# Second MLP product begun inside the first one's last pair, its second block product's loads and sums spread over steps

## The chip, the core and the metric

The kernel runs on one core of one Trainium2 chip, as one program and one launch. The metric is the device time of an execution in microseconds, taken as the median of several runs. The engines named below are TensorE (PE, matrix products), VectorE (DVE), ScalarE (ACT), GpSimd (POOL) and SyncE (SP), which issues all the DMAs that matter here.

## What is computed

The reference is a two-layer transformer trunk over 1024 latent tokens of width 1024 (an attention layer, then a gated-convolution layer). Each layer ends with the same kind of MLP, and the change lies in these two:

```python
def sq_relu_mlp(h, w1, w2):
    return jnp.square(jax.nn.relu(h @ w1)) @ w2

h = modulate(x, sh2, sc2)
x = layer_norm(DEEPNORM_ALPHA * x + g2 * sq_relu_mlp(h, mlp_w1[l], mlp_w2[l]), ln_g[l, 1], ln_b[l, 1])
```

Here `h` is 1024 x 1024, `w1` is 1024 x 4096 and `w2` is 4096 x 1024, all in float32.

## The kernel before

**Three matmuls for one.** Every product is made with operands split into a high part rounded to fp32r and a low part that is the rest. `mm3` (lines 72 to 75) issues high x high (line 73), one mixed product (line 74) and the other mixed product (line 75) into the same PSUM bank. A split is a cast on ACT (high part) and a subtraction on DVE (low part, line 78).

**Seven block products for eight.** Most of both MLP products is done by a Strassen-Winograd scheme: a 2 x 2 block product from seven block products, numbered x = 1 to 7, of sums of blocks.

**First product (`mlp_in`, line 721).** Four of the 32 row blocks of `w1` are multiplied plainly. The other 28 go in 14 pairs, p = 0 to 13. For each pair `quarters` (line 803) loads two row blocks, splits them, and runs the seven block products (n = 0 to 6, 12 matmuls each). After the squared ReLU, `mlp_in` stores the seven combinations that the second product needs in DRAM tensors `gq`, by DMAs at line 757. `between(n)` is called after each block product n.

**Second product (`merged`, line 860, called by `dense_out`).** It runs over seq: for x in the order 1, 6, 7, 4, 2, 5, 3, fourteen K tiles p = 0 to 13. One (x, p) is called a step here. A step is four times `mm3`, 12 matmuls of 128 x 512, into four PSUM banks (j = 0 to 3), in which all 14 steps of one x add up; x = 6 goes on in the banks of x = 1. `plus(x)` (line 925) then adds each of the four banks to the accumulator `acc`, once its last matmul is done. With x = 1 the fourteen steps are numbered 0 to 13 in this text, with x = 6 they are 14 to 27.

What a step needs is prepared two steps earlier by `ahead(n)`:

- `load` (line 894): 128 x 512 blocks of `w2` (256 KB): `a11`, `a21`, `a22`, later `a12`. Before step 0 `ahead(0)` asks for all 14 of `a11` and then all 28 of `a21` and `a22`.
- `make_b` (lines 903 to 906), for every second step: loads `b` from `gq` (512 KB, two K tiles) and splits it into `bh` (ACT, line 905) and `bl` (DVE, line 78).
- `make_a` (line 912): forms the block sum that this x wants (line 913), and splits it into two halves of a `part` tile: ACT cast at line 916, DVE subtraction at line 78. For x = 6 the sums are a21 = a11 - a21 and a22 = a22 - a21; x = 5 later wants a11 = a11 + a22.

`part`, `bh` and `bl` share a ring of six tiles with the split operands of `quarters`. Between `mlp_in` and `dense_out` the pool of temporaries changes (`small("x")`), whose tiles lie where the first product's temporaries were.

**What sets the order.** A tile scheduler places each engine's instructions in one queue per engine, as soon as it believes them ready, near the order in which the code issues them. Instructions wrapped in `keep_in_program_order` keep their places among each other: the casts and subtractions of `make_a` and `make_b` are wrapped, the block sums of line 913 are not. `high_priority(offset=60)` lets the four additions of `plus` move ahead. SP's queue holds all loads and stores. `gate_rows` (lines 195 to 206) is issued at step (2, 0): eight copies on DVE (`spread`, line 202) and eight PE transposes (line 203) that have no inputs from this product.

Of the kernel before, what the change touches and what calls it, by code (L numbers as in the profile page):

```python
# [55 lines left out]
class Trunk:  # L56
# [659 lines left out]
    def mlp(self, l, norm):  # L716
        self.g = [self.dp.tile([P, T], F32, name="g", tag="g", bufs=8) for _ in range(4)]
        self.gq = [{x: self.dp.tile([P, T], F32, name="gq", tag="gq", bufs=2 * 49) for x in range(1, 8)} for _ in range(7)]
        self.small("v")
        self.mlp_in(l)  # L720
        self.small("x")
        self.dense_out(self.w2[l], (self.m0, self.m1)[l], 40, norm)

    def mlp_in(self, l):

        nc = self.nc
        w1 = [self.weight(self.w1[l, m]) for m in range(4)]
        for h in range(2):  # L730
            for m in range(4):
                ps = self.gemm_in(w1[m], h * H2)
                r = self.tmp()
                nc.scalar.activation(r, ps, AF.Relu)
                nc.vector.scalar_tensor_tensor(out=r, in0=ps, scalar=0.0, in1=r, op0=ALU.max, op1=ALU.mult)
                self.leave(r, m, h)
                if h == 1:
                    self.combine(m)
        left = list(range(48)) if l == 0 else []
        if left:  # L740
            cb = self.raw("cb3")
            self.rows(cb, self.act[:, 0:8])

        def adaln():
            if left:
                i = left.pop(0)
                raw = self.raw()
                nc.sync.dma_start(out=raw, in_=self.adaT[1, i * P:(i + 1) * P, :])
                self.ada_dot(raw, cb, self.m1[:, i:i + 1], raw)
                if not left:  # L750
                    nc.vector.tensor_tensor(out=self.m1, in0=self.m1, in1=self.cols_t[:, C_ADAB + 48:C_ADAB + 96], op=ALU.add)

        for p in range(14):
            b = {}

            def leave(x, t):
                nc.sync.dma_start(out=self.gq[p // 2][x][:, p % 2 * H2:(p % 2 + 1) * H2], in_=t)

            def square(i, h, c, src):
                nc.scalar.activation(c, src, AF.Relu)  # L760
                nc.scalar.activation(c, c, AF.Square)
                b[i, h] = c
                if (i, h) != (0, 1):
                    leave({(0, 0): 1, (1, 0): 2, (1, 1): 3}[i, h], c)

            def between(n):
                if n % 2 == 1 or n == 6:
                    adaln()

            self.quarters([self.w1[l, 4 + 2 * p], self.w1[l, 5 + 2 * p]], square, between)  # L770

            def diff(a, c, op=ALU.subtract, out=None):
                out = out or self.tmp()
                nc.vector.tensor_tensor(out=out, in0=a, in1=c, op=op)
                return out

            b12 = diff(b[1, 1], b[0, 1], out=b[0, 1])
            leave(7, b12)
            b11 = diff(b[0, 0], b12, ALU.add)
            leave(6, b11)  # L780
            leave(5, diff(b[1, 1], b11))
            leave(4, diff(b[1, 0], b11))
# [91 lines left out]
    def merged(self, w, bs, k0, mod, gcol, step):  # L874

        nc = self.nc
        g = mod[:, gcol:gcol + 8]  # L880
        pairs = range(2 * len(bs))
# [27 lines left out]
                bparts[x, 2 * pp + i] = hi[:, c], lo[:, c]  # L909

        def make_a(x, p):
            for o, a, b, f in sums.get(x, ()):
                nc.vector.tensor_tensor(out=q[o, p], in0=q[a, p], in1=q[b, p], op=f)
            src = q[use[x], p]
            hi, lo = self.hl("part")
            self.tc.keep_in_program_order(nc.scalar.copy(out=hi, in_=src))  # L916
# [3 lines left out]
        def plus(x):  # L920

            for j, t in enumerate(ps[x]):
                jj, h = {1: (j, 0), 6: (j, 1), 7: (4 + j, 1), 4: (4 + j, 0), 2: (j, 0), 5: (4 + j, 1), 3: (j, 1)}[x]
                acc = self.acc[jj, h]
                nc.vector.scalar_tensor_tensor(out=acc, in0=t, scalar=g[:, jj:jj + 1], in1=acc, op0=ALU.mult, op1=ALU.add)

        def ahead(n):

            x, p = seq[n]
            if n == 0:  # L930
                for pp in pairs:
                    load("a11", pp)
                for pp in pairs:
                    load("a21", pp)
                    load("a22", pp)
            if x == 6:
                load("a12", p)
            if x == 4:
                load("a22", p, "a22r")
            if p % 2 == 0:  # L940
                make_b(x, p // 2)
            make_a(x, p)

        for n in range(-2, len(seq)):
            if n + 2 < len(seq):
                ahead(n + 2)
            if n < 0:
                continue
            x, p = seq[n]
            on = x in (6, 7, 4, 3)  # L950
            if p == 0:
# [13 lines left out]

    def dense_out(self, w, mod, gcol, norm):

        nc = self.nc

        def step(x, p):  # L970
# [3 lines left out]
                self.centre(norm[0], 0)  # L974

        if self.gq:
            self.merged(w, self.gq, len(self.g), mod, gcol, step)
        nchunk = len(self.g) // 4
        for c in range(nchunk):
            hid = {}  # L980
# [16 lines left out]
    def conv(self):  # L997
# [92 lines left out]
            self.quarters([self.cw_in[j], self.cw_in[j + 1]], gates)  # L1090
        self.small("x")
        self.gq = []
        self.dense_out(self.cw_out, self.m1, 16, (2, (self.m1, 3)))


class Attention:
# [202 lines left out]
class Grouped:  # L1299
# [154 lines left out]
    def ahead(self, j, m):  # L1454
        with self.t.tc.high_priority(offset=40):
            if m < 8:
                self.maximum(j, m // 2, m % 2)
            if m == 8:
                self.shifts(j)
# [58 lines left out]
```

## Time and profile before

| | before |
|---|---|
| median of 3 runs | 2580.47 us (2570.87 to 2581.67) |
| profiled execution, its own time | 2576.91 us |
| its span, first to last instruction | 2575.1 us |
| mean granted TensorE clock | 0.974 |
| PE busy / weight loads / DVE / ACT / POOL | 95% / 74% / 73% / 48% / 13% |

PE is busy for 95% of the span, so time can only be gained where PE waits or where its clock is granted at half. The table of 40 slices of the page shows such slices at several places: in the attention part, at the layer norms, and at the two changes from the first MLP product to the second (about 1200 to 1250 us in layer 0 and 2213 to 2252 us in layer 1). A granted clock of 1.00 is 2.4 GHz, the lower level is 1.2 GHz.

### The profile page before, as it was taken

The page shows a single profiled execution, that of the slowest core. Times are in us where ns is not written, and L with a number is a line of the kernel's source. Part 1 is how long each engine was busy: PE and PEld are TensorE (multiplying, and loading weights), DVE is VectorE, ACT ScalarE, POOL GpSimd, SP SyncE. Part 2 cuts the span into 40 slices and gives each one's busy share as a digit, 9 for nine tenths or more (in the row PEclk, how much of TensorE's full clock was granted, in tenths as well). Part 3 has the DMA queues.
Part 4 walks back from the last instruction along what each step waited for, and adds up shares of the span by engine and source line. Part 5 has one row for each costly group of instructions (what it writes and reads, how often), then busy time and mean ns, then how long its engine had stood idle before and what let it go on. Part 6 is the DMA issues. An engine that isn't in the chain of part 4 may idle for free. (4 is left out here: it accounts for less than half of the span.)

```text
span 2575.1 us, 30269 instructions
## 1 busy us (share of the span) xinstructions
PE 2435.0 (95%) x10950; PEld 1895.7 (74%) x10950; DVE 1891.7 (73%) x2925; ACT 1225.9 (48%) x1986; POOL 345.2 (13%) x230
## 2 busy tenths in 40 slices
PE   7999899999999979999899999999999999899997
PEld 5888677744447767787688777788777888688786
DVE  4847888887768787876756689767887565765867
ACT  3113577755542475554344346534258555344343
POOL 0001000044442410000000033001231000000002
PEclk9999899999999989999899999999999999899999
DMA  7811011000011057877542221123213444843231
GB/s 271 288 52 46 21 21 46 15 16 6 1 66 50 21 177 250 258 270 257 197 150 88 94 103 33 58 82 120 102 33 126 141 151 160 308 136 132 88 117 66
DMA packets 118519, 297.15 MB, mean 115 GB/s; under 512 B 13536, under 2 KB 19296, under 8 KB 118368
## 3 DMA queue, kind: packets, MB, share of 16 engines
q1 hardware_dynamic: 118368, 295.20, 34.2%
q8 instruction: 86, 1.41, 0.2%
q14 instruction: 65, 0.53, 0.1%
HBM read 225.29 MB, written 63.96 MB: 112 GB/s over the span
## 5 line engine op out<-in xcount | busy, mean ns | idle before, releaser
L74 PE MATMUL ps<-bl,part 128*128 128x512 f32 x784 | 309.7, 396 | 7.0 <-DVE bl L78 7.0
L73 PE MATMUL ps<-bh,part 128*128 128x512 f32 x784 | 310.4, 397 | 6.2 <-ACT part L916 6.2
L75 PE MATMUL ps<-bh,part 128*128 128x512 f32 x784 | 308.7, 396 | 5.8 <-DVE part L78 5.8
L916 ACT CAST part<-a 128x512 fp32r<-128x512 f32 x196 | 121.7, 623 | 306.5 <-PE ps L74 159.8
L78 DVE TENSOR_TENSOR part<-a,part 128x512 fp32r<-128x512 f32 x196 | 134.7, 690 | 162.1 <-ACT part L916 162.1
L73 PE MATMUL ps<-T,a 128*128 128x512 f32 x608 | 238.6, 392 | 6.4 <-DVE tmp L825 3.6
L74 PE MATMUL ps<-T,a 128*128 128x512 f32 x608 | 237.5, 391 | 2.2 <-DVE T L78 2.2
L75 PE MATMUL ps<-T,a 128*128 128x512 f32 x608 | 237.2, 390 | 0.0
L536 POOL TENSOR_TENSOR acc<-acc,mb 128x512 f32<-128x512 f32 x29 | 48.1, 1688 | 1070.6 <-ACT mb L533 1070.6
L73 PE MATMUL ps<-H,a 128*128 128x512 f32 x456 | 178.5, 392 | 3.7 <-ACT a L540 3.7
L74 PEld LDWEIGHTS ps<-bl,part 128*128 128x128 f32 x784 | 150.2, 192 | 41.1 <-DVE bl L78 9.2
L78 DVE TENSOR_TENSOR a<-raw,a 128x1024 fp32r<-128x1024 f32 (+1 forms) x114 | 119.2, 1047 | 83.3 <-PE ps L74 72.5
L75 PEld LDWEIGHTS ps<-bh,part 128*128 128x128 f32 x784 | 150.3, 192 | 38.7 <-DVE part L78 7.2
L73 PEld LDWEIGHTS ps<-bh,part 128*128 128x128 f32 x784 | 149.8, 191 | 39.3 <-ACT part L916 7.4
L74 PE MATMUL ps<-H,a 128*128 128x512 f32 x456 | 177.9, 390 | 0.0
L75 PE MATMUL ps<-H,a 128*128 128x512 f32 x456 | 177.7, 390 | 0.0
L540 ACT CAST a<-raw 128x1024 fp32r<-128x1024 f32 (+1 forms) x114 | 100.9, 908 | 136.2 <-PE ps L74 94.6
L825 DVE TENSOR_TENSOR tmp<-ps,tmp 128x512 f32<-128x512 f32 x114 | 78.4, 689 | 116.0 <-PE ps L75 80.2
L73 PEld LDWEIGHTS ps<-T,a 128*128 128x128 f32 x608 | 114.4, 188 | 35.3 <-DVE tmp L825 6.2
L74 PEld LDWEIGHTS ps<-T,a 128*128 128x128 f32 x608 | 114.4, 188 | 26.6 <-DVE T L78 3.6
L75 PEld LDWEIGHTS ps<-T,a 128*128 128x128 f32 x608 | 114.6, 188 | 23.9
L1390 ACT ACTIVATE pt<-s 128x512 f32<-128x512 f32 x160 | 92.7, 596 | 81.0 <-PE s L1389 72.1
(414 smaller groups left out, 5907.0 us busy)
## 6 DMA issues: line engine op xcount, KB each, us to landing
gq<-tmp SPq DMA_DIRECT2D x196, 256.0 KB, 3.4
b<-gq SPq DMA_DIRECT2D x98, 512.0 KB, 3.3
raw<-in_w SPq DMA_DIRECT2D x72, 512.0 KB, 4.2
a<-in_w SPq DMA_DIRECT2D x140, 256.0 KB, 5.1
raw<-in_adaT SPq DMA_DIRECT2D x48, 512.0 KB, 5.0
adar<-in_adaT SPq DMA_DIRECT2D x32, 512.0 KB, 5.0
raw<-in_cw_in SPq DMA_DIRECT2D x24, 512.0 KB, 3.6
ada<-in_adaN SPq DMA_DIRECT2D x16, 512.0 KB, 8.4
```

Source lines behind the costliest of these rows:

```text
L73: mm(ps, lhsT=lh, rhs=rh, start=start, stop=False, **kw)
L74: mm(ps, lhsT=lh, rhs=rl, start=False, stop=False, **kw)
L75: mm(ps, lhsT=ll, rhs=rh, start=False, stop=stop, **kw)
L78: return eng.tensor_tensor(out=out, in0=a, in1=hi.bitcast(F32), op=ALU.subtract)
L536: self.eng(NORM[li, h]["sub"][j]).tensor_tensor(out=a, in0=a, in1=mb, op=ALU.subtract)
L540: self.nc.scalar.copy(out=hi, in_=src)
L825: nc.vector.tensor_tensor(out=o, in0=a, in1=b, op=op)
L916: self.tc.keep_in_program_order(nc.scalar.copy(out=hi, in_=src))
L1390: nc.scalar.activation(pt[:, s, :], o, AF.Exp)
```

## The change

- `dense_out` and `merged` become generators. `merged` issues `ahead(0)` and `ahead(1)` and then yields; `mlp` runs it up to there from `between(5)` of the last pair (p = 13), and runs the rest after `small("x")`. The other caller of `dense_out`, in `conv`, runs it through at once.
- `ahead(0)` issues the 14 loads of `a11` alone. The loads of `a21` and `a22` for K tile p are issued by the step of x = 1 that prepares p.
- `make_b` is issued ahead of the loads in `ahead`.
- The difference a21 = a11 - a21 is issued by `differences`, wrapped in `keep_in_program_order`: one in each x = 1 step from p = 3 on, and one in each of the first x = 6 steps until none is left. The difference a22 = a22 - a21 is issued in `make_a` of x = 6 and is wrapped as well; the sum for x = 5 is not.

No instruction is added or removed; all of them move.

```diff
         self.small("v")
-        self.mlp_in(l)
+        out = self.dense_out(self.w2[l], (self.m0, self.m1)[l], 40, norm)
+        self.mlp_in(l, lambda: next(out))
         self.small("x")
-        self.dense_out(self.w2[l], (self.m0, self.m1)[l], 40, norm)
-
-    def mlp_in(self, l):
+        for _ in out:
+            pass
+
+    def mlp_in(self, l, then):
...
             def between(n):
                 if n % 2 == 1 or n == 6:
                     adaln()
+                if p == 13 and n == 5:
+                    then()
...
         def make_a(x, p):
-            for o, a, b, f in sums.get(x, ()):
-                nc.vector.tensor_tensor(out=q[o, p], in0=q[a, p], in1=q[b, p], op=f)
+            for o, a, b, f in sums.get(x, ())[x == 6:]:
+                i = nc.vector.tensor_tensor(out=q[o, p], in0=q[a, p], in1=q[b, p], op=f)
+                if x == 6:
+                    self.tc.keep_in_program_order(i)
...
+        early = []
+
+        def differences(n):
+
+            for _ in range(n):
+                p = early.pop(0)
+                o, a, b, f = sums[6][0]
+                self.tc.keep_in_program_order(nc.vector.tensor_tensor(out=q[o, p], in0=q[a, p], in1=q[b, p], op=f))
+
         def ahead(n):
 
             x, p = seq[n]
+            if p % 2 == 0:
+                make_b(x, p // 2)
             if n == 0:
                 for pp in pairs:
                     load("a11", pp)
-                for pp in pairs:
-                    load("a21", pp)
-                    load("a22", pp)
+            if x == 1:
+                make_a(x, p)
+                if p > 2:
+                    differences(1)
+                load("a21", p)
+                load("a22", p)
+                early.append(p)
+                return
             if x == 6:
                 load("a12", p)
+                if early:
+                    differences(1)
             if x == 4:
                 load("a22", p, "a22r")
-            if p % 2 == 0:
-                make_b(x, p // 2)
             make_a(x, p)
 
-        for n in range(-2, len(seq)):
+        for n in range(2):
+            ahead(n)
+        yield
+        for n in range(len(seq)):
             if n + 2 < len(seq):
                 ahead(n + 2)
-            if n < 0:
-                continue
...
         if self.gq:
-            self.merged(w, self.gq, len(self.g), mod, gcol, step)
+            yield from self.merged(w, self.gq, len(self.g), mod, gcol, step)
...
-        self.dense_out(self.cw_out, self.m1, 16, (2, (self.m1, 3)))
+        for _ in self.dense_out(self.cw_out, self.m1, 16, (2, (self.m1, 3))):
+            pass
```

The built programs differ only around the two changes from the first product to the second, and alike in both layers. Three places follow, all of layer 0.

ACT at the end of the first product, before: the last squared ReLUs of pair 13 (lines 760 and 761), then the casts for steps 0 to 2.

```order
L760 ACTIVATE tmp_10180<-tmp_10180 128x512
L761 ACTIVATE tmp_10180<-tmp_10180 128x512
L760 ACTIVATE tmp_10165<-tmp_10165 128x512
L761 ACTIVATE tmp_10165<-tmp_10165 128x512
L760 ACTIVATE tmp_10225<-ps_10121 128x512
L761 ACTIVATE tmp_10225<-tmp_10225 128x512
L905 CAST bh_10330<-b_10328 128x1024
L916 CAST part_10334<-a11_10244 128x512
L916 CAST part_10337<-a11_10246 128x512
```

ACT at the same place, changed (lines 762 and 763 are now the squared ReLU, 910 and 923 the casts).

```order
L762 ACTIVATE tmp_10180<-tmp_10180 128x512
L763 ACTIVATE tmp_10180<-tmp_10180 128x512
L910 CAST bh_10212<-b_10210 128x1024
L923 CAST part_10244<-a11_10216 128x512
L923 CAST part_10251<-a11_10218 128x512
L762 ACTIVATE tmp_10165<-tmp_10165 128x512
L763 ACTIVATE tmp_10165<-tmp_10165 128x512
L762 ACTIVATE tmp_10273<-ps_10121 128x512
L763 ACTIVATE tmp_10273<-tmp_10273 128x512
L910 CAST bh_10294<-b_10292 128x1024
```

The three casts for steps 0 and 1 now stand ahead of the last two squared ReLUs. On DVE the subtractions for steps 0 and 1 moved likewise, ahead of the last four combinations of the first product.

SP, the loads of `w2` blocks and of `b` for x = 1, before. `b_10416` is the `b` of steps 6 and 7; the `b` of steps 0 to 5 were issued earlier.

```order
L894 DMA a21_10324<-in_w2 128x512
L894 DMA a22_10326<-in_w2 128x512
L903 DMA b_10416<-gq_7644 128x1024
L903 DMA b_10452<-gq_7651 128x1024
L903 DMA b_10492<-gq_7658 128x1024
L903 DMA b_10528<-gq_7665 128x1024
L894 DMA a12_10564<-in_w2 128x512
```

SP at the same place, changed (line 899 loads blocks, line 908 loads `b`).

```order
L899 DMA a21_10371<-in_w2 128x512
L899 DMA a22_10373<-in_w2 128x512
L908 DMA b_10387<-gq_7644 128x1024
L899 DMA a21_10397<-in_w2 128x512
L899 DMA a22_10399<-in_w2 128x512
L899 DMA a21_10417<-in_w2 128x512
L899 DMA a22_10419<-in_w2 128x512
L908 DMA b_10433<-gq_7651 128x1024
```

The `b` of steps 6 and 7 stood behind all 28 loads of `a21` and `a22`; now it stands behind 12 of them, and each later `b` four loads further. Behind the first product's last five stores those are the last 25 before and 8 now.

DVE at the change from x = 1 to x = 6, before: the low part of step 14 (`part_10574`) stands ahead of the four additions of `plus(1)`, and the differences are long done; line 913 is by now the sum for x = 5.

```order
L78 TENSOR_TENSOR part_10549<-a11_10270,part_10549 128x512
L913 TENSOR_TENSOR a11_10270<-a11_10270,a22_10326 128x512
L78 TENSOR_TENSOR bl_10569<-b_10566,bh_10568 128x1024
L78 TENSOR_TENSOR part_10574<-a22_10274,part_10574 128x512
L925 SCALAR_TENSOR_TENSOR acc_6762<-ps_10349,m0_63,acc_6762 128x512
L925 SCALAR_TENSOR_TENSOR acc_6768<-ps_10350,m0_63,acc_6768 128x512
L925 SCALAR_TENSOR_TENSOR acc_6774<-ps_10351,m0_63,acc_6774 128x512
L925 SCALAR_TENSOR_TENSOR acc_6780<-ps_10352,m0_63,acc_6780 128x512
L78 TENSOR_TENSOR part_10593<-a22_10278,part_10593 128x512
```

DVE at the same place, changed (line 941 is the difference a21, line 918 the sums in `make_a`, line 932 `plus`).

```order
L941 TENSOR_TENSOR a21_10513<-a11_10238,a21_10513 128x512
L932 SCALAR_TENSOR_TENSOR acc_6762<-ps_10305,m0_63,acc_6762 128x512
L932 SCALAR_TENSOR_TENSOR acc_6768<-ps_10306,m0_63,acc_6768 128x512
L932 SCALAR_TENSOR_TENSOR acc_6774<-ps_10307,m0_63,acc_6774 128x512
L932 SCALAR_TENSOR_TENSOR acc_6780<-ps_10308,m0_63,acc_6780 128x512
L918 TENSOR_TENSOR a22_10249<-a22_10249,a21_10247 128x512
L918 TENSOR_TENSOR a11_10216<-a11_10216,a22_10249 128x512
L78 TENSOR_TENSOR part_10585<-a22_10249,part_10585 128x512
L941 TENSOR_TENSOR a21_10539<-a11_10240,a21_10539 128x512
L918 TENSOR_TENSOR a22_10256<-a22_10256,a21_10254 128x512
L918 TENSOR_TENSOR a11_10218<-a11_10218,a22_10256 128x512
L78 TENSOR_TENSOR part_10604<-a22_10256,part_10604 128x512
```

The sum and the low part of step 14 now stand behind the four additions, and every x = 6 step has two block sums in the queue ahead of its low part. Behind these rows come the `bl` of steps 16 and 17, the last difference a21, and the sum a22 of step 16. On PE the eight transposes of `gate_rows` stood together between steps 5 and 6; four of them still do, the other four now stand between steps 13 and 14.

## Rows read from the trace of the kernel before

**Rows 1.** Busy time by stretch: us, PE, PEld, DVE, ACT, POOL, PEclk, DMA share, GB/s.

```profile
1200.00:1225.00 25.00, 22.00 (x84) 16.88 (x82) 20.94 (x33) 8.85 (x13) 0.00 (x0) 0.86 1.01 356
1225.00:1250.00 25.00, 17.31 (x58) 12.77 (x59) 20.75 (x37) 6.38 (x9) 0.00 (x0) 0.73 0.68 258
```

**Rows 2.** Timeline of PE, both product changes: start, length, line, tiles, count [idle before, releaser].

```profile
1201.90 0.39 PE L75 MATMUL ps<-T,a 128*128 128x512 f32 x1
1205.09 1.65 PE L73 MATMUL ps<-bh,part 128*128 128x512 f32 x3 [2.80 <-ACT part L916]
...
1213.71 0.39 PE L73 MATMUL ps<-bh,part 128*128 128x512 f32 x1
...
2213.66 0.39 PE L75 MATMUL ps<-T,a 128*128 128x512 f32 x1
...
2224.62 0.39 PE L73 MATMUL ps<-bh,part 128*128 128x512 f32 x1
```

**Rows 3.** Timeline of ACT and DVE at the end of layer 0's first product.

```profile
1198.33 0.63 ACT L761 ACTIVATE tmp<-tmp 128x512 f32<-128x512 f32 x1
1200.33 0.63 ACT L760 ACTIVATE tmp<-tmp 128x512 f32<-128x512 f32 x1 [1.37 <-DVE tmp L825]
...
1204.42 1.13 ACT L916 CAST part<-a 128x512 fp32r<-128x512 f32 x2
...
1199.61 0.69 DVE L825 TENSOR_TENSOR tmp<-ps,tmp 128x512 f32<-128x512 f32 x1 [1.97 <-PE ps L75]
1201.66 1.42 DVE L774 TENSOR_TENSOR tmp<-tmp 128x512 f32<-128x512 f32 x2 [1.36 <-ACT tmp L761]
```

**Rows 4.** Timeline of PE at the second gap, and behind it.

```profile
1224.60 0.28 PE L203 MATMUL one<-ident,spread 128*128 128x128 f32 x1
1227.20 0.33 PE L203 MATMUL one<-ident,spread 128*128 128x128 f32 x1 [2.33 <-DVE spread L202]
...
1235.77 0.79 PE L74 MATMUL ps<-bl,part 128*128 128x512 f32 x1 [3.77 <-DVE bl L78]
...
1241.98 0.40 PE L73 MATMUL ps<-bh,part 128*128 128x512 f32 x1
...
1260.39 0.39 PE L73 MATMUL ps<-bh,part 128*128 128x512 f32 x1
...
1298.47 0.39 PE L73 MATMUL ps<-bh,part 128*128 128x512 f32 x1
...
2271.03 0.39 PE L73 MATMUL ps<-bh,part 128*128 128x512 f32 x1
```

**Rows 5.** Timeline of SP's queue, ACT and DVE at the second gap.

```profile
1206.06 16.73 SPq L894 DMA_DIRECT2D a<-in_w  x25
...
1229.21 1.05 ACT L905 CAST bh<-b 128x1024 fp32r<-128x1024 f32 x1 [9.47 <-DMA b<-gq]
...
1220.91 6.10 DVE L913 TENSOR_TENSOR a<-a,a 128x512 f32<-128x512 f32 x10
...
1234.50 1.21 DVE L78 TENSOR_TENSOR bl<-b,bh 128x1024 fp32r<-128x1024 f32 x1
```

**Rows 6.** The loads of tile b, 1200 to 1262 us.

```profile
DMA to landing us min/median/max: 3.2/4.8/8.4
```

**Rows 7.** Timeline of DVE at the change from x = 1 to x = 6.

```profile
1258.52 0.69 DVE L78 TENSOR_TENSOR part<-a,part 128x512 fp32r<-128x512 f32 x1 [0.39 <-ACT part L916]
1259.13 2.72 DVE L925 SCALAR_TENSOR_TENSOR acc<-ps,m,acc 128x512 f32<-128x512 f32 x4
1261.77 0.68 DVE L78 TENSOR_TENSOR part<-a,part 128x512 fp32r<-128x512 f32 x1
```

**Rows 8.** Timeline of PE behind two waits elsewhere.

```profile
1024.67 0.50 PE L73 MATMUL ps<-T,a 128*128 128x512 f32 x1 [1.65 <-DVE tmp L825]
...
1431.94 1.21 PE L75 MATMUL ps<-bh,part 128*128 128x512 f32 x4 [2.64 <-DVE part L78]
...
1436.62 0.39 PE L73 MATMUL ps<-bh,part 128*128 128x512 f32 x1
```

## Prediction, made before the changed kernel was run

> **What bounds it now.** Read first the busy shares: PE is busy for 95% of the span, so only its waits and its half-clock stretches can be won. The busy time by stretch shows both at the change from the first MLP product to the second: from 1200 to 1250 us PE works 39.3 of 50 us, at a granted clock of 0.86 and then 0.73, while no other engine is full for the whole stretch [rows 1]. The timeline of PE says what ended each wait.
>
> Fix the price of undisturbed work first. From step 14 to step 28 PE runs 168 matmuls in 1298.47 - 1260.39 = 38.08 us without a wait [rows 4]: 0.227 us a matmul, 2.72 us a step.
>
> The first gap: the last matmul of layer 0's first product starts at 1201.90, so steps 0 and 1 could be over, and step 2 begin, at 1201.90 + 0.23 + 5.44 = 1207.57. Step 2 begins at 1213.71, 6.14 us late; in layer 1 the same sum gives 2224.62 - 2219.33 = 5.29 us [rows 2]. PE waits 2.80 us for ACT's cast of `part`, and then runs its first steps at the lower clock level, 1.2 GHz (three matmuls in 1.65 us [rows 2]).
>
> The second gap: twelve steps of 2.72 us after step 2, step 14 should begin at 1246.35; it begins at 1260.39, 14.04 us late, and in layer 1 at 2271.03 instead of 2257.26, 13.77 us late [rows 2, 4]. Before step 6 PE waits for `spread` copies and then 3.77 us for `bl`, and the clock is back only at 1241.98 [rows 4]. Two things stand behind it. SP issues 25 block loads from 1206.06 on, for 16.73 us, and only then the `b` of step 6, whose cast starts at 1229.21 [rows 5]. And when that cast is done (1230.26), DVE is at its list of differences (ten in 6.10 us from 1220.91, then more): `bl` starts at 1234.50, 4.2 us later [rows 5].
>
> Together: 6.14 + 5.29 + 14.04 + 13.77 = **39.2 us** in which the two changes of product are slower than PE alone. That is the most that this change can win, and it holds the eight gate transposes of each layer.
>
> **Steps 0 and 1 early.** It moves a cast of `b`, two of `part`, and their three subtractions. ACT is free from 1198.33 + 0.63 = 1198.96 and idles 1.37 us before 1200.33 [rows 3]. `bh` (1.05 us [rows 5]) ends at 1200.0, the two `part` (1.13 us for two [rows 3]) at 1201.2. DVE is free at 1199.61 + 0.69 = 1200.3 [rows 3]: `bl` (1.21 us [rows 5]) to 1201.5, two low parts (0.69 us each [rows 7]) to 1202.1 and 1202.7. Step 0 is due at 1202.13 and needs its low part only at its third matmul, 0.45 us in; step 1 is due at 1204.85. All are in time, at no cost to PE. What they push back: the last squared ReLU on ACT by some 0.9 us, and the last four combinations on DVE, which start about 1202.7 instead of 1201.66 [rows 3]. Behind these wait the last five `gq` stores and, in SP's queue, the block loads; both ended about 1206 and still do, since the one difference that stood between the combinations has moved out. Steps 2 and 3 need no new transfer: their `b` was issued before. So the whole first gap goes: **-11.4 us** over both layers.
>
> **Loads interleaved.** Behind the five stores, the `b` of step 6 waits for 8 block loads instead of 25. At 16.73 / 25 = 0.67 us each [rows 5] it is issued by 1206.06 + 5.4 = 1211.4; `b` loads take 3.2 to 8.4 us to land there, median 4.8 [rows 6]: 1216.2. With 1.05 us of cast, 1.21 of `bl` and 0.69 of low part, 1219.2. Step 6 is due at 1202.13 + 6 x 2.72 = 1218.45, plus the four transposes ahead of it, and wants the low part after some 0.5 us more. I take 0; the ends are 0 and, with 8.4 us to land, about 2 us a layer. Later `b` gain on PE: four blocks and a `b` are 1.5 MB, 4.0 us at the 392 GB/s that 25 x 256 KB in 16.73 us make, against 5.44 us for two steps.
> The Trainium skill speaks against so many small loads: "DMA: Bandwidth & Descriptors", section Bandwidth, gives 341 GB/s for a 1 MB transfer and asks for at least that size. By it the 2.6 MB up to that `b` would take about 1 us longer, an estimate, and the gain would be some 2 us less over both layers; the trace, with 392 GB/s from 256 KB loads [rows 5], disagrees.
>
> **Sums spread.** With the differences kept in order, `bl` finds at most one sum (0.61 us) ahead of it, and the rest of the second gap goes: -27.8 us. But the spreading makes new costs, per layer:
>
> - The transposes. Four now run between steps 5 and 6: 0.28 us each at full clock [rows 4], overlapping, so 0.7 to 1.1 us; I take 0.9. The other four fall into the wait of the next point.
> - Step 14. On DVE the sum a22 of step 14 is now behind the four additions of `plus(1)`. Let step 13 start at 0. Its third matmul ends the first bank: 2 x 0.227 + 0.39 = 0.85, so the additions start about 0.89. Four of them hold DVE for 1261.77 - 1259.13 = 2.64 us [rows 7]: 3.53. The sum ends at 4.22 (0.69), the cast (0.62, with 0.05 for each handover) at 4.89, and step 14 starts at 4.94 instead of 2.72: 2.2 us. Before, the same place cost nothing, since low part and sum were ready ahead of the additions [rows 7].
> - Step 16. DVE goes on with the low part of step 14 (from 4.93), then, each 0.61 later, a difference, a sum and a sum for x = 5, then a low part, then `bl`, which waits for the cast of `b` on ACT (to 8.46) and ends at 9.72, a difference, and the sum of step 16 at 10.25 to 10.94. Its cast ends at 11.60; step 16 was due at 4.94 + 5.44 = 10.38 and starts at 11.65: 1.3 us.
> - The rest of x = 6. Per two steps the chain is sum 0.69, cast 0.62, cast of `b` up to 1.0 behind it, `bl` 1.14, sum 0.69, cast 0.62, low part 0.61, about 5.5 us with handovers, against 5.44 on PE: it holds, no more. 0.05 a pair, 0.3 us. Two sums more a step have no row of before at full pace, so 0 to 2 us.
>
> From x = 7 on no sums are left and the order is the old one. New costs: 0.9 + 0 + 2.2 + 1.3 + 0.3 = 4.7 us a layer, 9.4 us in all.
>
> **The sum.** -39.2 + 9.4 = **-29.8 us**. From the profiled execution's 2576.9 us that makes 2547.1; the median shown is 3.6 us above that execution, which makes 2550.7. I say 2549 us.
>
> **Rivals.** *The clock falls at the new waits.* A wait of 1.65 us left the next matmul at 0.50 us and no more; one of 2.64 us was followed by 13 matmuls in 1436.62 - 1431.94 = 4.68 us instead of 2.95 [rows 8], 1.7 us lost. The new waits of about 1.4 us (step 14, behind its transposes) and 1.3 us (step 16) lie near the first, but two in a row are not in the rows. If each drops the clock, 4 x 1.7 = 6.9 us go: 2556; with the late `b` as well, 2560.
> The Trainium skill, "Perfetto Trace Analysis", section Matmul Optimizations, says that the engine "dynamically scales power based on utilization" and wants matmuls back to back in batches; by that rule these waits cost as in this rival. The trace agrees with it for the long wait and not for the short one [rows 8].
>
> *The early casts don't run early.* Should their ring tiles come free only with the last block product, ACT would stand there and the first gap stay: gain 18.4, 2560 us. Against it: the operand of block product 5 is done when DVE reads its bank at 1199.61 [rows 3], and that frees the tile needed.
>
> *Slower than before: sums, casts and subtractions run as one chain through x = 1 and x = 6.* If nothing overlaps, two steps take 2 x (0.69 + 0.62 + 0.69) + 1.05 + 1.21 + 0.3 of handovers = 6.6, with waits of casts behind the wrong sum some 6.9 us. It decides from 5.44 + 39.2 / 28 = 6.84 us, the 28 pairs of both x in both layers sharing what is won. With the transposes and step 14 on top (6.2 us) it ends at about 2580 to 2585. For it: DVE keeps its written order, as `bl` at 1234.50 shows. Against: the low part does not wait for the sum that follows it, and ACT's cast of `b` runs beside DVE.
>
> **Chances and range.** Forecast 0.75, clock 0.15, early casts late 0.06, chain 0.04. What a measurement of this kernel can tell from no change is about 0.5%, 13 us. All cases but the last are faster than that unless two of them meet: faster 0.93, same 0.05, slower 0.02 (the chain with a fallen clock). The range goes from no cost at step 16 and behind it (gain 33, 2543.5) and a baseline some us lower, as the runs of before vary by 10, to the clock's case: 2539 to 2561.
>
> **What would show it.** Right: no idle time ahead of step 0 and clock 1.00 there; no wait for `bl` over 2 us near step 6; a wait on ACT's cast (its releaser, DVE's sum) of 2.2 us from the end of step 13, in part filled by four transposes; one of about 1.3 us two steps later. From the end of the first product to step 28: 76.2 + 4.7 = 81 us a layer, against 1298.47 - 1202.13 = 96.3 in layer 0 now. Wrong: a `b` that lands late at step 6, half clock behind step 14, or waits at every second x = 6 step, which would mean that DVE's chain is longer than 5.5 us.

## The result and the profile after

The changed kernel takes 2550.74 us (median of 4 runs, 2547.37 to 2552.53); the kernel before, run beside it, 2578.65 us (now the median of 4 runs). The ratio is 0.9894, 95% interval 0.9879 to 0.9909: 28 us less. Forecast were 2549 us and a gain of 29.8 us. The profiled execution took 2547.37 us, its span is 2545.6 us and its mean granted clock 0.983.

The busy time of the two stretches of [rows 1], after the change (us, PE, PEld, DVE, ACT, POOL, PEclk, DMA share, GB/s):

```profile
1200.00:1225.00 25.00, 24.32 (x110) 19.77 (x109) 18.40 (x33) 11.16 (x17) 0.00 (x0) 1.00 1.01 357
1225.00:1250.00 25.00, 22.89 (x102) 18.37 (x100) 20.76 (x30) 8.36 (x12) 0.00 (x0) 1.00 0.93 351
```

PE works 47.2 of 50 us where it worked 39.3, and the clock is 1.00 in both where it was 0.86 and 0.73. DVE is no busier than before (39.2 us against 41.7), and in the first stretch the DMA engines move as much (357 GB/s against 356): only the order is another.

The timeline of PE in layer 1, at the places of [rows 2, 4]: the last matmul of the first product and step 0, the four transposes and step 6, the four others and step 14, step 16, step 28 (start, length, line, tiles, count, in brackets the idle time before and its releaser):

```profile
2197.47 0.39 PE L75 MATMUL ps<-T,a 128*128 128x512 f32 x1
2197.70 0.39 PE L73 MATMUL ps<-bh,part 128*128 128x512 f32 x1
...
2214.03 0.60 PE L203 MATMUL one<-ident,spread 128*128 128x128 f32 x4
2214.54 0.98 PE L73 MATMUL ps<-bh,part 128*128 128x512 f32 x3
...
2236.53 0.60 PE L203 MATMUL one<-ident,spread 128*128 128x128 f32 x4
2238.86 0.50 PE L73 MATMUL ps<-bh,part 128*128 128x512 f32 x1 [1.74 <-ACT part L923]
...
2245.64 0.49 PE L73 MATMUL ps<-bh,part 128*128 128x512 f32 x1 [0.98 <-ACT part L923]
...
2279.45 0.39 PE L73 MATMUL ps<-bh,part 128*128 128x512 f32 x1
```

Step 0 follows the last matmul of the first product by 0.23 us, one matmul: nothing is left of the first gap. Step 6 has only its transposes ahead of it. Two waits are new, both for ACT's cast of `part`, at steps 14 and 16. They are the only ones that the table of waits names from the change of product to step 28 of layer 1 (waiting for, us in total, times, longest):

```profile
PE ps L73 <- ACT part L923: 2.7, 2, 1.7
```

Layer 0 has a third one, ahead of step 6: in the first row SP issues eight block loads, in the second the `b` of step 6, in the third ACT gets to its cast, in the last PE to the step.

```profile
1206.07 5.30 SPq L899 DMA_DIRECT2D a<-in_w  x8
1211.65 0.38 SPq L908 DMA_DIRECT2D b<-gq  x1
...
1217.86 1.05 ACT L910 CAST bh<-b 128x1024 fp32r<-128x1024 f32 x1 [4.50 <-DMA b<-gq]
...
1219.48 0.73 PE L73 MATMUL ps<-bh,part 128*128 128x512 f32 x2 [0.68 <-ACT part L923]
```

**One measure for all kernels.** Below, the *lateness* of a layer is the time from the end of the first product (start of its last matmul + 0.23 us) to the first matmul of step 28, less 28 x 2.72 = 76.16 us. The start of step 28 is found by counting twelve matmuls a step on PE's timeline. The sums are of unrounded times. Each lateness comes from one profiled execution; of the two kernels that were profiled twice, one differs by 0.5 us between its traces and the other by 1.0. In three kernels some of the eight transposes stand behind step 28 and so outside this measure: seven with the loads spread and nothing else (they cost 0.8 us a layer there), three with the sums not kept (0.4), one with `b` earlier (0.2). Each kernel ran beside runs of the kernel before, and the ratio compares with those.

| kernel | lateness, layer 0 + layer 1, us | median us | ratio to before, 95% interval |
|---|---|---|---|
| before | 20.2 + 19.1 = 39.2 | 2577 to 2579 | 1 |
| after | 6.4 + 5.6 = 12.0 | 2550.74 | 0.9894 (0.9879 to 0.9909) |
| after, second time | 6.1 + 5.4 = 11.5 | 2553.35 | 0.9911 (0.9896 to 0.9927) |
| early only | 17.4 + 17.2 = 34.5 | 2573.87 | 0.9989 (0.9977 to 1.0001) |
| early and order, loads at once | 18.7 + 19.4 = 38.1 | 2577.46 | 1.0000 (0.9990 to 1.0011) |
| spread only | 8.6 + 7.3 = 15.9 | 2557.68 | 0.9926 (0.9908 to 0.9943) |
| loads spread, nothing else | 6.0 + 4.8 = 10.7 | 2550.19 | 0.9900 (0.9883 to 0.9918) |
| early and loads, sums not kept | 2.2 + 2.8 = 5.0 | 2543.37 | 0.9878 (0.9855 to 0.9902) |
| sums for x = 5 kept | 5.5 + 6.3 = 11.8 | 2561.49 | 0.9948 (0.9934 to 0.9961) |
| seven sums early | 1.2 + 2.4 = 3.6 | 2542.95 | 0.9872 (0.9859 to 0.9886) |
| seven sums early, second time | 1.8 + 2.8 = 4.6 | 2545.98 | 0.9880 (0.9863 to 0.9896) |
| both | 2.1 + 3.0 = 5.1 | 2553.14 | 0.9908 (0.9895 to 0.9922) |
| seven sums early, `b` earlier | 0.9 + 1.2 = 2.1 | 2542.73 | 0.9869 (0.9855 to 0.9884) |

The lateness fell by 39.2 - 12.0 = 27.2 us; the two profiled executions differ by 29.5. The rest lies outside the two changes of product, where executions of one and the same kernel differ more than that: from step 28 of layer 0 to the end of layer 1's first product the first trace of the changed kernel takes 913.3 us, the second 919.5.

### The profile page after: what moved, and what is told of

Same layout as the page of the kernel before. It is cut to its first block, busy times and chain, and to the rows that moved or that the text cites. A ratio compares the mean times of both kernels' runs of the same rounds, so it can differ in the third digit from the quotient of the medians.

```text
span 2545.6 us, 30261 instructions
## 1 busy us (share of the span) xinstructions
PE 2420.8 (95%) x10950; PEld 1885.3 (74%) x10950; DVE 1895.4 (74%) x2925; ACT 1229.6 (48%) x1986; POOL 346.3 (14%) x230
## 5 line engine op out<-in xcount | busy, mean ns | idle before, releaser
L73 PE MATMUL ps<-bh,part 128*128 128x512 f32 x784 | 306.8, 392 | 6.1 <-ACT part L923 6.1
L75 PE MATMUL ps<-bh,part 128*128 128x512 f32 x784 | 304.8, 392 | 5.8 <-DVE part L78 5.8
L536 POOL TENSOR_TENSOR acc<-acc,mb 128x512 f32<-128x512 f32 x29 | 48.1, 1690 | 1043.3 <-ACT mb L533 1043.3
L75 PEld LDWEIGHTS ps<-bh,part 128*128 128x128 f32 x784 | 147.6, 189 | 40.1 <-DVE part L78 9.4
L73 PEld LDWEIGHTS ps<-bh,part 128*128 128x128 f32 x784 | 147.3, 188 | 39.8 <-ACT part L923 9.3
L78 DVE TENSOR_TENSOR bl<-b,bh 128x1024 fp32r<-128x1024 f32 x98 | 119.9, 1223 | 23.0 <-ACT bh L910 22.6
```

The source lines that it names most:

```text
L73: mm(ps, lhsT=lh, rhs=rh, start=start, stop=False, **kw)
L75: mm(ps, lhsT=ll, rhs=rh, start=False, stop=stop, **kw)
L78: return eng.tensor_tensor(out=out, in0=a, in1=hi.bitcast(F32), op=ALU.subtract)
L536: self.eng(NORM[li, h]["sub"][j]).tensor_tensor(out=a, in0=a, in1=mb, op=ALU.subtract)
```

## Experiments: which part carries the gain

**Early only.** The changed kernel without the spreading: steps 0 and 1 early, the 28 loads at once, no sum in a kept order.

```diff
 (in ahead, x == 1)
-                if p > 2:
-                    differences(1)
-                load("a21", p)
-                load("a22", p)
 (behind the first yield)
+        for pp in pairs:
+            load("a21", pp)
+            load("a22", pp)
 (in make_a, all sums again, not kept in order)
```

> Steps 0 and 1 are emitted within the first product's last pair as in the changed kernel, but the loads of a21 and a22 and the block sums are left as in the kernel before (28 loads at once, ahead of the b of step 6, and no kept order for the sums). If the two parts add up, as the prediction's sum has it, the first gap of 11.4 us over both layers goes and the second stays: gain 11 us, about 2567 us. The rival: the second gap is fixed in absolute time by SP's queue of block loads (the b of step 6 still lands about 1229 us) and by DVE's list of sums, so the early start only lengthens the wait ahead of step 6: step 0 starts about 1202, step 6 not before 1235 as now, gain 0 to 3 us, 2576 to 2579 us.

Measured: 2573.87 us against 2578.49, and the ratio of the comparison, 0.9989, has 1 in its interval. The rival holds. The timelines of layer 0 (SP, ACT, DVE, PE) show what fixes step 6:

```profile
1206.25 16.31 SPq L899 DMA_DIRECT2D a<-in_w  x24
1222.91 3.08 SPq L908 DMA_DIRECT2D b<-gq  x5
...
1228.99 1.04 ACT L910 CAST bh<-b 128x1024 fp32r<-128x1024 f32 x1 [15.68 <-DMA b<-gq]
...
1222.71 9.11 DVE L918 TENSOR_TENSOR a<-a,a 128x512 f32<-128x512 f32 x15
1231.74 1.22 DVE L78 TENSOR_TENSOR bl<-b,bh 128x1024 fp32r<-128x1024 f32 x1
...
1230.61 0.79 PE L73 MATMUL ps<-bh,part 128*128 128x512 f32 x1 [7.43 <-ACT part L921]
1233.01 0.79 PE L74 MATMUL ps<-bl,part 128*128 128x512 f32 x1 [1.61 <-DVE bl L78]
```

The first gap is gone (step 2 is on time to 0.01 us), but the cast of the `b` of step 6 starts at 1228.99, as it did before (1229.21 [rows 5]). It hangs on SP's queue, and that did not move. PE came to step 6 earlier and waited longer: 29.4 us from the end of the first product to step 6, before 29.1. What is gained is 4.7 us of 39.2. Most of it comes from `bl`, which now finds less of the list of sums ahead of it: PE waits 1.61 us for it, before 3.77 [rows 4].

**Early and order, loads at once.** The changed kernel with the 28 loads put back behind the first yield, sums kept in order.

```diff
-                load("a21", p)
-                load("a22", p)
 (behind the first yield)
+        for pp in pairs:
+            load("a21", pp)
+            load("a22", pp)
```

> The changed kernel with its loads of a21 and a22 put back into one block of 28 ahead of the b of step 6; sums kept in order, steps 0 and 1 early. Theory: the place of b in SP's queue costs by itself: b of step 6 lands about 1229 us, bl ends about 1231.5, step 6 was due about 1219.5, so PE waits about 12 us per layer and then runs at half clock for some us, less what the later waits at steps 14 and 16 lose when DVE has caught up (3 us): 2571 to 2575 us. Rival (the sums in DVE's queue were the whole second gap): no wait over 2 us ahead of step 6, 2551 to 2555 us.

Measured: 2577.46 us, no gain at all, and the wait sits where the theory puts it:

```profile
1230.03 1.04 ACT L910 CAST bh<-b 128x1024 fp32r<-128x1024 f32 x1 [14.98 <-DMA b<-gq]
...
1231.65 0.80 PE L73 MATMUL ps<-bh,part 128*128 128x512 f32 x1 [10.71 <-ACT part L923]
```

The size was too hopeful by some 4 us: step 6 starts 11.8 us late, as expected, but step 6 itself then takes 5.73 us instead of 2.72 at the fallen clock, and the waits behind step 13 (0.70 and 1.16 us of idle PE at steps 15 and 16) cost 3.9 us a layer, 1 us less than in the changed kernel and not 3. Early start and kept order together are worth nothing while `b` stands behind the loads. This run also parts the two things behind the second gap: no sum stands ahead of `bl` here, and step 14 is still 14.8 and 15.6 us late in the two layers, against 17.4 and 17.2 in the run with the early start alone. So the place of `b` makes nearly all of it, and the list of sums some 2 us a layer.

**Spread only.** The changed kernel with `self.mlp_in(l, lambda: None)`: nothing early.

> Loads spread and sums kept in order as in the changed kernel, but steps 0 and 1 are not emitted early. By the prediction's terms the second gap of 27.8 us goes, the new costs of 9.4 us come, and the first gap of 11.4 us stays: gain 18 us, about 2560 us, with the wait of 2.8 us for ACT's cast ahead of step 0 still there. The rival (the parts do not add up): the late start gives the b of step 6 and the sums more time, so no wait ahead of step 6, and the gain is larger by up to 2 us; or the fallen clock after the first gap slows PE so far that DVE's chain keeps up and the waits at steps 14 and 16 are the same, 2.3 and 1.2 us.

Measured: 2557.68 us, 2 us under the forecast. The wait of 2.81 us for ACT's cast ahead of step 0 is there, but step 2 is late by 4.7 and 3.1 us only (before 6.14 and 5.29), since less ran at the lower clock: it was granted at 0.57 and 1.00 in the 4 us behind that wait, before at 0.51 and 0.72 in the 6 us behind it. No wait at step 6, as the rival's first half says. Without the early start the scheduler put the sum of step 14 ahead of `plus(1)`, so the waits behind it are smaller (0.16 us at step 15, 1.15 at step 16).

**Loads spread, nothing else.** The kernel before with one part alone: the loads of a21 and a22 in the steps of x = 1, `make_b` ahead of them; nothing early, no sum in a kept order.

> The kernel before with one part of the change alone: the loads of a21 and a22 spread over the steps of x = 1 and issued behind the b of the step; steps 0 and 1 not early, no block sum in a kept order. Theory after the first runs: the place of b in SP's queue is the whole second gap, and the kept order of the sums costs instead of helping. Then this one part is worth more than everything else together: the first gap stays (4.7 and 3.1 us in the run with the spread alone), no wait at steps 6, 14 and 16: some 7 to 8 us above the kernel with early steps and no kept order (2543.4 us), 2550 to 2552 us, no slower than the whole change. Rival: without the early start and the kept order the sums bunch up ahead of bl, as in the kernel before (4 us of wait a layer and a fallen clock): 2560 us or more.

Measured: 2550.19 us. This one part is worth as much as the whole change (2550.74 and 2553.35). All that is left of its lateness is the first gap, 5.6 and 4.5 us, whose beginning reads as in [rows 2], and 0.3 us in step 14, where one transpose stands:

```profile
1204.06 0.96 PE L73 MATMUL ps<-bh,part 128*128 128x512 f32 x3 [2.80 <-ACT part L921]
1205.66 1.32 PE L74 MATMUL ps<-bl,part 128*128 128x512 f32 x3 [0.64 <-DVE bl L78]
```

PE does not wait at steps 6, 14 and 16, with no sum in a kept order: the rival falls. So the second gap goes when `b` stands ahead of the loads and these are spread, with nothing else changed, and the early start pays only behind that.

## Experiments: what the new waits are

**Early and loads, sums not kept.** The changed kernel with the block sums and differences left to the scheduler.

```diff
-            for o, a, b, f in sums.get(x, ())[x == 6:]:
-                i = nc.vector.tensor_tensor(out=q[o, p], in0=q[a, p], in1=q[b, p], op=f)
-                if x == 6:
-                    self.tc.keep_in_program_order(i)
+            for o, a, b, f in sums.get(x, ()):
+                nc.vector.tensor_tensor(out=q[o, p], in0=q[a, p], in1=q[b, p], op=f)
...
-                if p > 2:
-                    differences(1)
...
-                if early:
-                    differences(1)
```

> The changed kernel with the block sums out of the kept order: the scheduler moves most of them up into x = 1, so that several stand ahead of the bl of step 6 and nearly all sums of x = 6 are done before plus(1). If the kept order is what makes the change work: bl of step 6 waits for up to four sums as before, 2 to 4 us a layer plus a fallen clock, 2555 to 2562 us. Rival: since the loads are spread, the sums cannot bunch up, bl loses at most 1 us, and the waits at steps 14 and 16 (2.3 and 1.2 us a layer) shrink because the sums are done early: 2543 to 2549 us.

Measured: 2543.37 us; the rival holds. The waits at steps 14 and 16 are gone and the lateness is 5.0 us, in which step 6 of layer 1 still waits 1.1 us for its late `b`. With the loads spread, the sums cannot bunch up ahead of `bl`, and the scheduler has done the sums of the first x = 6 steps by the time of `plus(1)`. The kept order, which the prediction needed for the second gap, costs 6 to 7 us of lateness. (The times alone would not show it: the ratios 0.9878 and 0.9894 have intervals that overlap. The next run, with the changed kernel beside it, does.)

**Seven sums early.** The changed kernel, order still kept, with the first seven sums a22 moved from x = 6 into the last seven steps of x = 1. It ran beside a second run of the changed kernel.

```diff
+                if x == 6 and p < 7:
+                    continue
                 i = nc.vector.tensor_tensor(out=q[o, p], in0=q[a, p], in1=q[b, p], op=f)
...
             if x == 1:
                 make_a(x, p)
                 if p > 2:
                     differences(1)
+                if p >= 7:
+                    e = p - 7
+                    self.tc.keep_in_program_order(nc.vector.tensor_tensor(
+                        out=q["a22", e], in0=q["a22", e], in1=q["a21", e], op=sub))
```

> The changed kernel once more, as the yardstick for the three kernels that run beside it on the same chip. Expected 2547 to 2553 us, with the waits at step 14 and step 16 of each layer as in its first trace (about 1.73 and 0.97 us of idle PE).

> The changed kernel with the first seven sums a22 of x = 6 moved up into the last seven steps of x = 1 (kept in order; no other change). Theory: the wait ahead of step 14 is the sum of step 14 behind plus(1) in DVE's queue, and the wait at step 16 is what DVE has not made up by then. With the sums done, the casts of steps 14 to 20 wait for nothing on DVE: both waits of PE for ACT's cast go (2.3 and 1.2 us a layer), a wait of at most 1 us for the low part of step 14, still behind plus(1), takes the first one's place: 4 to 6 us less than the changed kernel, 2544 to 2547 us. Rival: DVE's queue as a whole is too long at this place, so that five more block sums in x = 1 (up to 2.4 us of DVE work a step of 2.72 us) make new waits there, and the wait only moves: within 2 us of the changed kernel.

Measured: 2553.35 us (2547.59 to 2557.91) for the changed kernel and 2542.95 us (2542.10 to 2544.44) for this one. The theory holds, and the gain is larger than the 4 to 6 us expected. First DVE and ACT of the changed kernel at step 14 of layer 1 (step 13 starts at 2233.81), then DVE, ACT and PE of this one at step 14 of layer 0:

```profile
2234.69 2.79 DVE L932 SCALAR_TENSOR_TENSOR acc<-ps,m,acc 128x512 f32<-128x512 f32 x4
2237.40 1.41 DVE L918 TENSOR_TENSOR a<-a,a 128x512 f32<-128x512 f32 x2
...
2238.19 0.62 ACT L923 CAST part<-a 128x512 fp32r<-128x512 f32 x1 [5.55 <-DVE a L918]
```

```profile
1239.26 2.72 DVE L934 SCALAR_TENSOR_TENSOR acc<-ps,m,acc 128x512 f32<-128x512 f32 x4
1241.89 0.69 DVE L943 TENSOR_TENSOR a<-a,a 128x512 f32<-128x512 f32 x1
1242.49 0.69 DVE L78 TENSOR_TENSOR part<-a,part 128x512 fp32r<-128x512 f32 x1
...
1238.42 0.62 ACT L925 CAST part<-a 128x512 fp32r<-128x512 f32 x1 [1.37 <-PE ps L75]
...
1242.76 0.60 PE L203 MATMUL one<-ident,spread 128*128 128x128 f32 x4
1243.23 1.20 PE L75 MATMUL ps<-bh,part 128*128 128x512 f32 x4
```

In the first, the cast of step 14 waits 5.55 us for a sum that DVE starts only after four additions. In the second the sum is done, the cast waits for PE alone and starts ahead of the additions, and step 14 starts on time, 2.72 us after step 13. Its low part (1242.49) still stands behind the additions, and PE fills that time with the other matmuls of the step and four transposes. The twelve steps from step 16 on take 32.64 us, 2.72 each: the rest of x = 6, 1.2 us a layer, went too, which the expectation had not counted. The lateness is 7.9 us less than that of the changed kernel beside it; the medians differ by 10.4, of which the rest is not in these stretches.

**Sums for x = 5 kept, and both edits.** The changed kernel with `if x in (6, 5):` ahead of `keep_in_program_order`, so that the sums a11 + a22 run in x = 5; and the same on top of the seven early sums.

> The changed kernel with the sums for x = 5 kept in order too, so that they leave x = 6 and run in x = 5 itself (no other change). The wait at step 14 (2.3 us a layer) must stay: its sum is still behind plus(1). If DVE's queue length is what makes step 16 and the rest of x = 6 late (1.2 and 1.2 us a layer), one block sum of 0.61 us a step less removes both: 4 to 5 us less than the changed kernel, 2546 us. If it is the chain of sum, cast, cast of b, bl, sum, cast (about 5.5 us for two steps) that binds, each step still needs its own sum first, and the gain is 0 to 1 us: 2549 to 2551 us.

> Both edits at once: seven sums a22 early, and the sums for x = 5 out of x = 6. If sums behind plus(1) and DVE's load in x = 6 are all that the changed kernel lost behind step 13, steps 13 to 28 run at 2.72 us each but for the low part of step 14 behind plus(1) (up to 1 us): 7 to 8 us less than the changed kernel, 2542 to 2544 us, about as fast as the kernel with the sums out of the kept order (2543.4 us). If it is no faster than the better of the two single edits, the two edits remove the same wait.

Measured: 2561.49 and 2553.14 us, each some 8 to 10 us *slower* than the kernel without that edit. At the change of product nothing happens: the waits at steps 14 and 16 are 1.73 and 0.98 us as before, and the twelve steps from step 16 on take 33.74 us against 33.75. So one block sum less per step on DVE does not shorten x = 6: the chain binds there, not DVE's load. In the changed kernel the sum for x = 5 runs while DVE waits for ACT's cast anyway (the rows of x = 6 in the next section); without it DVE idles 0.74 to 0.77 us ahead of each low part instead of 0.02 to 0.05. The loss is in x = 5, whose fourteen steps take 49.0 and 48.9 us in the two layers instead of 43.6 and 45.3 (with both edits 49.2 and 49.2). DVE, ACT and PE in layer 0, first of the kernel with the x = 5 sums kept, then DVE and PE of the changed kernel beside it (L536 is `centre`, issued at step (5, 2)):

```profile
1410.92 5.87 DVE L536 TENSOR_TENSOR acc<-acc,mb 128x512 f32<-128x512 f32 x6 [1.05 <-ACT mb L533]
1416.71 0.68 DVE L918 TENSOR_TENSOR a<-a,a 128x512 f32<-128x512 f32 x1
...
1417.42 0.62 ACT L923 CAST part<-a 128x512 fp32r<-128x512 f32 x1 [6.54 <-DVE a L918]
...
1418.09 0.79 PE L73 MATMUL ps<-bh,part 128*128 128x512 f32 x1 [5.10 <-ACT part L923]
```

```profile
1412.37 5.90 DVE L536 TENSOR_TENSOR acc<-acc,mb 128x512 f32<-128x512 f32 x6 [1.90 <-ACT mb L533]
1418.20 0.68 DVE L78 TENSOR_TENSOR part<-a,part 128x512 fp32r<-128x512 f32 x1
...
1418.93 1.63 PE L75 MATMUL ps<-bh,part 128*128 128x512 f32 x4 [2.63 <-DVE part L78]
```

It is the pattern of step 14 again: a block sum behind a row of additions, and the cast behind the sum. The wait of 2.63 us becomes 5.10 (layer 1: 3.10 and 5.54), and the clock behind it is granted at 0.51 from 1418 to 1424 us instead of 0.72. Neither expectation had looked at x = 5.

**Seven sums early, `b` earlier.** Every `b` loaded two steps earlier, with the seven early sums; the kernel with the seven sums alone ran beside it.

```diff
-            raw = self.raw("b")
-            nc.sync.dma_start(out=raw, in_=bs[pp][x])
+            raw = raws.pop(0)
...
             if p % 2 == 0:
+                load_b(n + 2)
                 make_b(x, p // 2)
```

Not shown: `load_b`, which asks for a raw tile, issues its load and appends it to `raws`, and its first call at n = 0.

> The kernel with seven sums a22 early, and every b loaded two steps earlier, so that the b of step 6 has four block loads fewer ahead of it in SP's queue (about 2.5 us). If step 6's rest of wait (0 to 0.9 us of idle PE a layer, and three matmuls at half clock) is that b landing late, it goes: stretch from the end of the first product to step 28 of 77 us in both layers, 1 to 2 us less than the kernel with seven sums early that runs beside it, 2541 to 2542 us. Rival: the block loads pushed back behind b come late for the differences and sums of x = 1, or the raw tiles run out: same time or a few us slower.

> The kernel with seven sums a22 early, as before, beside the two others: 2541 to 2545 us.

Measured: 2542.73 us (2540.30 to 2545.21) against 2545.98 (2539.73 to 2550.30). The times cannot be told apart, the traces can. The queue of SP, ACT and PE ahead of step 6 in layer 0:

```profile
1209.22 2.29 SPq L899 DMA_DIRECT2D a<-in_w  x4
1211.55 0.43 SPq L912 DMA_DIRECT2D b<-gq  x1
...
1218.24 1.05 ACT L918 CAST bh<-b 128x1024 fp32r<-128x1024 f32 x1 [1.58 <-DMA b<-gq]
...
1221.51 0.39 PE L73 MATMUL ps<-bh,part 128*128 128x512 f32 x1
```

Step 6 is due at 1221.51 here (the product ends at 1205.19) and starts then; the table of waits of PE is empty from there to step 28 in both layers. The lateness is 2.1 us, with seven of the eight transposes in it: this is the end of what this place can give.

## Why the prediction was right, and where it was not

**What bounds, and the 39.2 us.** Right: with all waits removed the lateness fell from 39.2 to 2.1 us, and nothing else had to move.

**Steps 0 and 1 early, -11.4 us.** Right as a term: step 2 is on time to 0.01 us in both layers. But it was summed as a part that stands by itself, and it does not: alone it lowered the lateness by 4.7 us and the time by nothing that can be told. It pays once `b` no longer fixes step 6: the early start takes 10.7 - 5.0 = 5.7 us of lateness from the kernel with the loads spread and the sums not kept, less than 11.4, since step 6 is then due earlier and `b` becomes late for it.

**Loads interleaved.** The issue of `b` was forecast for 1211.4 and came at 1211.65. Its landing was forecast for 1216.2 from the median of 4.8 us; ACT had it at 1217.86, 6.2 us after the issue. So the late `b` cost 0.68 us of idle PE in layer 0 and none in layer 1, within its ends (0 to 2), not the 0 that was taken. (By its own terms the late end was too low: with 8.4 us to land the low part is there at 1222.8, nearly 3 us after PE wants it.) By the rule of the Trainium skill for larger transfers ("DMA: Bandwidth & Descriptors", section Bandwidth) the issue would have come about 0.8 us later, an estimate (eight loads, 2.1 MB, at 341 instead of 392 GB/s); it came 0.25 us later than the row of before had it, so the trace stays nearer to the row than to the rule.

**Sums spread, -27.8 us.** The gain came, the reason was half wrong. The prediction had the kept order of the differences as what lets `bl` start; the runs show that spreading the loads behind `b` does it, and that keeping the order costs. That step failed: "With the differences kept in order, `bl` finds at most one sum (0.61 us) ahead of it". That is true, and not needed.

**The new costs.** In layer 1, where each step can be read off PE's timeline:

| term | forecast, us | measured, us |
|---|---|---|
| transposes between steps 5 and 6 | 0.9 | 0.5, and 0.2 more in steps 6 and 7 |
| late `b` | 0 | 0 (layer 0: 0.68 idle) |
| wait at step 14 | 2.2 | 2.3, and 0.1 more in step 14 itself |
| wait at step 16 | 1.3 | 1.2 |
| rest of x = 6 | 0.3 | 1.2 |
| sum | 4.7 | 5.6 |

The chain behind step 14 was followed right: the four additions start 0.88 us after step 13 (forecast 0.89), the sum at 3.59 (3.53), step 14 at 5.05 (4.94). Mis-sized is the rest of x = 6. The chain was the one forecast, whose listed terms add up to 5.37 us, taken as 5.5 with handovers. The rows of DVE and of ACT's casts of `part` and `b` show the whole period, from one block sum behind `bl` to the next:

```profile
2249.76 1.42 DVE L918 TENSOR_TENSOR a<-a,a 128x512 f32<-128x512 f32 x2
2251.22 0.69 DVE L78 TENSOR_TENSOR part<-a,part 128x512 fp32r<-128x512 f32 x1
2251.82 1.41 DVE L918 TENSOR_TENSOR a<-a,a 128x512 f32<-128x512 f32 x2
2253.26 0.69 DVE L78 TENSOR_TENSOR part<-a,part 128x512 fp32r<-128x512 f32 x1
2254.21 1.23 DVE L78 TENSOR_TENSOR bl<-b,bh 128x1024 fp32r<-128x1024 f32 x1 [0.26 <-ACT bh L910]
2255.35 1.41 DVE L918 TENSOR_TENSOR a<-a,a 128x512 f32<-128x512 f32 x2
...
2250.56 0.63 ACT L923 CAST part<-a 128x512 fp32r<-128x512 f32 x1 [1.97 <-DVE a L918]
2252.60 0.62 ACT L923 CAST part<-a 128x512 fp32r<-128x512 f32 x1 [1.42 <-DVE a L918]
2253.13 1.05 ACT L910 CAST bh<-b 128x1024 fp32r<-128x1024 f32 x1
```

The second of each two sums is the one for x = 5; it runs beside the cast that the low part waits for. The period is 5.59 us, so the handovers take 0.22 us and not 0.13. Against 5.44 on PE that is 0.15 us a pair instead of 0.05, 0.9 of the 1.2 us, and it comes out in PE's rows as first matmuls of up to 0.50 us, not as named waits. Over both layers the new costs were 12.0 us instead of 9.4. That the median came within 2 us of the forecast all the same is in part luck: it is owed to the rounding to 2549 and to the 2.3 us gained outside the stretches, which vary by more.

**The rivals.** The clock did not fall: granted 1.00 from 2238 to 2243 and from 2245 to 2250 us, behind the waits of 1.74 and 0.98 us; one matmul of 0.50 us follows each. The rule of the Trainium skill, "Perfetto Trace Analysis", section Matmul Optimizations, that TensorE's power is scaled by its utilization, agrees with most of the long waits of the other kernels (below) and not with these two. The early casts did run early: step 0 follows the first product at once. The chain is real, as the rows above show, but at 5.59 us a pair it is far from the 6.84 from which the change would have lost.

## What to carry to other kernels

When two stalls follow each other, ask for the second one's release in absolute time. Here a queue fixed it: removing the first stall alone gained nothing that could be told, and removing the second alone gained as much as the whole change. Before an order is kept by hand, look at what stands behind a row of additions: a sum whose cast is waited for must be ahead of it (step 14, and `centre` in x = 5). An operation that looks like a load on a stage may be there because the next stage is fuller; taking the x = 5 sums out of x = 6 cost 8 and 10 us over the two layers.

## What was not expected of the hardware

- What follows a wait is not settled by its length alone. Behind 0.98 to 1.74 us the clock stayed at 1.00, and one matmul took 0.50 instead of 0.39 us. Behind 2.81 and 2.80 us, the same wait ahead of step 0 in the two layers of the kernel with the spread alone, it was granted at 0.57 and at 1.00 over the next 4 us. Behind 7.43 and 1.61 us (early only) it was 0.50, or 1.2 GHz, from 1230 to 1237 us and 0.99 from 1237 to 1250.
- Which of the repeated executions of one kernel is shown matters at this size: the changed kernel's medians were 2550.74 and 2553.35 us, and 6.2 us between its two traces lie in one stretch (from step 28 of layer 0 to layer 1's second product) that the change does not touch. Set side by side, matmul by matmul, the traces part mainly where PE waits: about 1.5 us in x = 5 of layer 0, and 4.6 at 1784 to 1788 us of the first trace, where PE's one wait is 0.83 us; in the second it is 2.94 us and matmuls of 0.60 to 0.63 us follow. Why these waits differ from one execution to the next stays open.
